# The first stage of a hybrid encoder layer: K taken by halves, four row tiles in six PSUM banks, part of the modulation as columns

## The chip, the cores and the metric

The kernel runs on one core of one Trainium2 chip. The metric is the device time of one execution in microseconds (us). Three runs of the kernel before gave 2279.6, 2280.0 and 2279.08 us; their median is 2279.6 us.

## The reference

One layer of an encoder on a sequence of 2048 rows of width 1024 (D), in float32:

```python
mod = jax.nn.silu(c) @ w_mod + b_mod              # (1, 6*1024): one row for the whole sequence
shift1, scale1, gate1, shift2, scale2, gate2 = split(mod, 6)
hmix = rms_norm(x, g_norm1) * (1.0 + scale1) + shift1
proj = hmix @ w_in          # 2832 columns: attention q, k, v, mLSTM q, k, v, o, 16 gates
...                         # banded attention, bidirectional mLSTM, output projection, gated SwiGLU FFN
```

The change concerns the first three lines and a part of the fourth: of the columns of `w_in` the first stage makes those that are wanted with rows on the partitions, the 128 of the attention's v, the 16 gates and the 512 of the mLSTM's v, 656 in all. Everything after that is the same in both kernels.

## The kernel before, in words

The 2048 rows are 16 row tiles of 128, in four groups of four (`n` from 0 to 3). A group's four x tiles are squared and summed on ACT (`squares`), their root is taken on DVE (`rsqrt`, 12 small instructions), and they are scaled by it (`scaled`). Then the group is turned: for each of the eight slices `k` of 128 columns, PE transposes four 128x128 blocks into one PSUM bank, ACT multiplies by the norm's gain and scale and adds the shift (`gs1`, `mod[:, 0, :]`, one value per partition), and DVE splits the result in a high part (float32r, rounded) and a low part, the rest (`turned`, `turned_split`). `hT[n]` holds both parts.

A product of two float32 numbers is made of three float32r matmuls: high by high, high by low, low by high (`mm3`, lines 56 to 58). `w_in`'s 656 columns are split in the same way into `wh` and `wl` (`load_nat`, `split_nat`), in two halves of K: z = 0 is k 0 to 3, z = 1 is k 4 to 7. A row tile needs 656 float32 columns of PSUM, more than the 512 of a bank, so it takes two banks, `pa` with 272 columns and `pv` with 384. A bank is named by a tag: "g", "a" and "c" have two banks each, "b" and "d" one. `nat_mm` makes one row tile: for each of the two banks, all k of its range, three matmuls each.

The modulation is needed as columns, one value per partition and k. `load_mod(m, z)` loads 512 columns of `w_mod` as four pieces of 512 KB, each with two k. `mod_sum` multiplies them by silu(c), the column `sc_col`. With `n_pe` = 4, PE takes k 0 to 3 with `sc_col` as the stationary operand, which gives one row of 512 (line 220); DVE sums k 4 to 7 in `acc`; PE adds the sum over the partitions of `acc` (line 221); ACT copies the row out (line 223), and PE turns it into four columns (line 226). With `n_pe` = 0, DVE sums all eight k and PE makes the columns from `acc` at once (line 230). `mod_bias` adds b_mod, `scales` makes `gs1`.

The order around the change: PE's instructions stay as written. ACT's, DVE's, POOL's and SP's stay as written inside the block that `pre` opens; after `pre.close()` a planner places them, and it may put later work ahead of instructions of that block where it sees them idle. SP issues nearly all loads and stores in one order, with at most eight under way. In that block, group 0 is squared, scaled and turned, in this order: modulation (1, 0) and (0, 0), `w_in`'s first half, turns of k 0 to 3, the first half of K for row tiles 0, 1 and 2 (six banks), then modulation (1, 1) and (0, 1), `w_in`'s second half, and turns of k 4 to 7. The loop over groups follows: row tiles 0 to 2 do their second half of K, and row tile 3 all of it, with a turn of group 1 after every second of its 16 steps; in group 1 a turn of group 2 stands after every eighth step. `EVERY` holds these distances. After each row tile ACT and DVE empty its banks into `vs` (one buffer, the attention's v in both parts) and `va` (two buffers), and SP stores these. `mod_row(m)`, a generator, makes the other four modulation rows; `next(vecs)` takes one half of such a row after each row tile. From line 498 on the stage with the other columns of `w_in` follows.

Of the kernel before, what the change touches and what calls it, by code (L numbers as in the profile page):

```python
# [11 lines left out]
F32 = mybir.dt.float32  # L12
F32R = mybir.dt.float32r
# [8 lines left out]
P = 128  # L22
# [14 lines left out]
def hybrid_layer_kernel(  # L37
# [125 lines left out]
    def squares(pl, xt):  # L163

        ssq = pl.tile([P, 4], F32, tag="ssq", name="ssq")
        for i in range(4):
            jk = pl.tile([P, D], BF16, tag="junk", name="junk", bufs=1)
            act.activation(jk, xt[i], AF.Square, accum_out=ssq[:, i:i + 1])
        return ssq
# [22 lines left out]

    wm_slots = deque(range(8, 16))

    def load_mod(m, z):

        r = []
        for k in range(0, KT, 2):
            w = big(wm_slots[0], "wmod", (P, 2, 512), F32)
            wm_slots.rotate(-1)  # L200
            sp.dma_start(w, w_mod[k * P:(k + 2) * P, m * D + z * 512:m * D + (z + 1) * 512]
                         .rearrange("(k p) c -> p k c", p=P))
            r.append(w)
        return r

    def mod_sum(pl, m, z, ws_, n_pe):


        acc = pl.tile([P, 512], F32, tag="macc", name="macc")
        for k in range(n_pe, KT):  # L210
            w = ws_[k // 2][:, k % 2, :]
            if k == n_pe:
                dve.tensor_scalar(acc, w, sc_col[:, k:k + 1], None, MUL)
            else:
                dve.scalar_tensor_tensor(acc, w, sc_col[:, k:k + 1], acc, MUL, ADD)
        yield True
        if n_pe:
            ps = bank("b", "modrow")
            for k in range(n_pe):
                pe.matmul(ps[:1, :], sc_col[:, k:k + 1], ws_[k // 2][:, k % 2, :], start=k == 0, stop=False)  # L220
            pe.matmul(ps[:1, :], ones[:, 0:1], acc, start=False, stop=True)
            row = pl.tile([1, 512], F32, tag="mrow", name="mrow", bufs=1)
            act.activation(row, ps[:1, :], AF.Copy)
            ps = bank("b", "modps")
            for k in range(4):
                pe.matmul(ps[:, k:k + 1], row[:, k * P:(k + 1) * P], ones[:1, 0:1], start=True, stop=True)
        else:
            ps = bank("d", "modps")
            for k in range(4):
                pe.matmul(ps[:, k:k + 1], acc[:, k * P:(k + 1) * P], ones[:, 0:1], start=True, stop=True)  # L230
        yield True
        mod_bias(m, z, ps)
        yield True

    def mod_bias(m, z, ps):
        o = O_BM + m * KT + 4 * z
        dve.tensor_tensor(mod[:, m, 4 * z:4 * z + 4], ps[:, :4], cols[:, o:o + 4], ADD)
# [40 lines left out]
    with tc.tile_pool(name="sw", bufs=2, side="right", reuse_waits="tile") as sw:  # L278
# [19 lines left out]
        wm = {(m, 0): load_mod(m, 0) for m in (1, 0)}  # L298
# [28 lines left out]
        def scales(z):  # L327
            dve.scalar_tensor_tensor(gs1[:, BD[z]], mod[:, 1, BD[z]], 1.0, cols[:, O_G1 + 4 * z:O_G1 + 4 * z + 4], ADD, MUL)

# [10 lines left out]
        def split_nat(z, r):  # L340
            ks = BD[z]
            act.activation(wh[:, ks, :144], r[0], AF.Copy)
            dve.tensor_tensor(wl[:, ks, :144], r[0], wh[:, ks, :144].bitcast(F32), SUB)
            for i in range(4):
                k, v = 4 * z + i, r[1 + i // 2][:, i % 2]
                act.activation(wh[:, k, 144:], v, AF.Copy)
                (pool, dve)[i % 2].tensor_tensor(wl[:, k, 144:], v, wh[:, k, 144:].bitcast(F32), SUB)
# [55 lines left out]

        wn = [load_nat(0)]
        wm[1, 1] = load_mod(1, 1)
        wn.append(load_nat(1))
        wm[0, 1] = load_mod(0, 1)
        xts += [load_x(1), load_x(2)]
        for src, o, n in ((g_norm2, O_G2, 8), (conv_b, O_CB, 8), (conv_w[0], O_CW, 24), (g_attn_out, O_GA, 4), (g_mlstm_out, O_GM, 4)):
            sp.dma_start(rows[1][o - N_A:o - N_A + n, :], src.rearrange("o (a b) -> (o a) b", b=P))  # L410
        hT.append(Kt(0, "hT0"))
        ms = {(m, z): mod_sum(s1, m, z, wm[m, z], 4 if m == 1 - z else 0) for z in range(2) for m in (1, 0)}
        ssq = squares(s1, xts[0])
        r = rsqrt(s1, ssq, 4, D, "rs")
        next(ms[1, 0])
        scaled(xts[0], r, True)
        next(ms[0, 0])
        next(ms[1, 0])
        next(ms[1, 0])
        next(ms[0, 0])  # L420
        next(ms[0, 0])
        scales(0)
        split_nat(0, wn[0])
        ops = {i: (bank("gga"[i], "pa"), bank("acc"[i], "pv")) for i in range(3)}
        for k in range(4):
            turned_split(s1, xts[0], k, gs1, mod[:, 0, :], hT[0])
        for i in range(3):
            deque(nat_mm(0, i, *ops[i], range(4)), 0)
        next(ms[1, 1])
        split_nat(1, wn[1])  # L430
        next(ms[1, 1])
        next(ms[1, 1])
        next(ms[0, 1])
        next(ms[0, 1])
        next(ms[0, 1])
        scales(1)
        for k in range(4, KT):
            turned_split(s1, xts[0], k, gs1, mod[:, 0, :], hT[0])
        pre.close()
        gn = cp.tile([P, 2, 2, HM, NT], F32, name="gn")  # L440
        bgv = bg.rearrange("p (d y h) -> p y d h", d=2, y=2)
        vecs = iter(())
        EVERY = ((0, 0, 0, 2), (8, 8, 8, 8), (2, 0, 0, 0), (0, 0, 0, 0))
        for n in range(NB):
# [3 lines left out]
            if n == 0:  # L448
                xts.append(load_x(3))
# [1509 lines left out]
```

## Time and profile before

| | |
|---|---|
| median of three runs | 2279.6 us |
| profiled execution: its time, its span | 2281.54 us, 2279.7 us |
| PE, DVE, ACT, POOL busy | 98%, 71%, 46%, 47% of the span |
| first matmul of the first stage (line 56) | 28.34 us |
| first matmul of row tile 4 | 78.21 us |
| first transpose inside row tile 8 | 111.98 us |
| first matmul of the next stage (line 498) | 180.92 us |

The span is the time from the first to the last instruction; the execution's own time is 1.8 us longer. Times in rows are counted from the start of the span. A row of an order in time has the start, the length, the engine, the line, the operation, what it writes and reads, its shape and the number of instructions merged into it; in square brackets stands how long the engine sat idle before it and what ended that. PEld is the loading of matmul weights, which overlaps PE. The granted clock is the share of TensorE's full clock that the chip let it have.

### The profile page before, as it was taken

The numbers are of one execution on the slowest core, as the hardware profiler recorded it, in microseconds if no ns is written. First come the engines' busy times: TensorE is split into PE (matmuls) and PEld (weight loads), VectorE is DVE, ScalarE is ACT, GpSimd is POOL, SyncE is SP. The second block draws the span as 40 slices with busy tenths as digits, with TensorE's granted clock in tenths as the row PEclk, the third lists the DMA queues.
The fourth block names the chain that finished last, engine by engine and source line by source line (L and its number), as shares of the span: only waits on it lengthen the run. The fifth ranks groups of instructions, "written<-read, shape, count | busy, mean of one in ns | idle before, by whom it ended". The sixth has DMA issues, their size and how long they took to land.

```text
span 2279.7 us, 32432 instructions
## 1 busy us (share of the span) xinstructions
PE 2225.9 (98%) x10822; PEld 1858.6 (82%) x10822; DVE 1610.1 (71%) x2931; ACT 1059.1 (46%) x2206; POOL 1067.4 (47%) x927
## 2 busy tenths in 40 slices
PE   7999999999999999999999999999999999999998
PEld 4997888888888878778888888788888888888886
DVE  6787577656688887786667786666667666785694
ACT  4433555544677746354445444433333333233352
POOL 1006535334344344436656665656566654692020
PEclk8999999999999999999999999999999999999999
DMA  8576755585666575764343454533333374442462
GB/s 323 167 246 218 231 170 163 186 242 171 201 186 183 173 251 197 265 223 147 111 157 111 157 180 147 172 98 111 97 111 97 111 253 144 166 152 93 145 216 93
DMA packets 352811, 391.28 MB, mean 172 GB/s; under 512 B 21260, under 2 KB 251004, under 8 KB 352644
## 3 DMA queue, kind: packets, MB, share of 16 engines
q1 hardware_dynamic: 352420, 389.18, 52.0%
q8 instruction: 85, 1.39, 0.2%
q14 instruction: 82, 0.67, 0.1%
q10 hardware_dynamic: 224, 0.04, 0.0%
HBM read 269.95 MB, written 119.19 MB: 171 GB/s over the span
## 4 chain that ended last, share of the span: by engine, by line
PE 51%; DVE 3%; DMA 2%; issue 1%; ACT 1%; POOL 1%; SPq 0%; ACTq 0%; DVEq 0%; POOLq 0%
PE fp L56 11%; PE fp L57 11%; PE fp L58 11%; PE fo L58 5%; PE fo L57 5%; PE fo L56 5%; PE ops L56 1%; DMA al<-a_d 1%; PE ops L58 1%; PE ops L57 1%; DVE ra L1858 1%; DVE w L1728 0%; DVE al L1719 0%; PE trn L183 0%; DMA B<-hop_d 0%
## 5 line engine op out<-in xcount | busy, mean ns | idle before, releaser
L498 PE MATMUL gps<-hT,whi 128*128 128x512 f32 x1088 | 396.2, 419 | 0.3 <-DVE cacc L513 0.3
L57 PE MATMUL fo<-w,ah 128*128 128x512 f32 x616 | 239.8, 389 | 1.6 <-DVE w L1728 1.6
L58 PE MATMUL fo<-w,al 128*128 128x512 f32 x616 | 239.8, 389 | 0.3 <-DVE al L1719 0.3
L56 PE MATMUL fo<-w,ah 128*128 128x512 f32 x616 | 239.7, 389 | 0.0
L498 PE MATMUL gps<-hT,wlo 128*128 128x512 f32 x544 | 226.6, 416 | 0.0
L498 PEld LDWEIGHTS gps<-hT,whi 128*128 128x128 f32 x1088 | 199.8, 190 | 24.4 <-DVE cacc L513 0.7
L56 PE MATMUL fp<-T,S 128*128 128x512 f32 x528 | 206.9, 392 | 2.9 <-ACT s L1615 2.9
L57 PE MATMUL fp<-T,S 128*128 128x512 f32 x528 | 205.7, 390 | 0.0
L58 PE MATMUL fp<-T,S 128*128 128x512 f32 x528 | 205.4, 389 | 0.0
L1719 DVE TENSOR_TENSOR al<-al,ah 128x1024 fp32r<-128x1024 f32 x77 | 116.8, 1521 | 112.9 <-ACT ah L1718 112.7
L1718 ACT ACTIVATE ah<-al 128x1024 fp32r<-128x1024 f32 x77 | 81.6, 1060 | 188.9 <-DMA al<-a_d 183.7
L1458 DVE TENSOR_TENSOR S<-sf,S 128x512 fp32r<-128x512 f32 x86 | 129.6, 1545 | 39.4 <-ACT S L1457 39.2
L1458 DVE TENSOR_TENSOR A<-graw,A 128x512 fp32r<-128x512 f32 x86 | 129.4, 1526 | 14.5 <-ACT A L1457 14.5
L1623 DVE SCALAR_TENSOR_TENSOR g<-t,g 128x512 f32<-128x512 f32 x44 | 44.2, 1005 | 132.6 <-ACT t L1622 132.6
L57 PEld LDWEIGHTS fo<-w,ah 128*128 128x128 f32 x616 | 115.6, 188 | 26.2 <-DVE w L1728 2.0
L58 PE MATMUL fp<-B,A 128*128 128x512 f32 x352 | 136.9, 389 | 0.0
L56 PE MATMUL fp<-B,A 128*128 128x512 f32 x352 | 136.9, 389 | 0.0
L57 PE MATMUL fp<-B,A 128*128 128x512 f32 x352 | 136.9, 389 | 0.0
L58 PEld LDWEIGHTS fo<-w,al 128*128 128x128 f32 x616 | 115.6, 188 | 24.7 <-DVE al L1719 0.7
L56 PEld LDWEIGHTS fo<-w,ah 128*128 128x128 f32 x616 | 115.6, 188 | 24.0
L1462 POOL TENSOR_TENSOR sf<-A,A22r 128x512 f32<-128x512 f32 x43 | 61.3, 1427 | 154.8 <-DMA A22r<-in_w_ffn_in_dram 121.2
L798 POOL TENSOR_SCALAR ap<-ap,adn 128x384 f32<-128x384 f32 (+1 forms) x128 | 71.1, 574 | 123.3 <-PE atp L805 62.8
(418 smaller groups left out, 6168.5 us busy)
## 6 DMA issues: line engine op xcount, KB each, us to landing
al<-a_d SPq DMA_DIRECT2D x77, 512.0 KB, 3.7
wmod<-in_w_mod_dram SPq DMA_DIRECT2D x48, 512.0 KB, 7.6
graw<-in_w_ffn_in_dram SPq DMA_DIRECT2D x43, 512.0 KB, 3.7
a_d<-ka SPq DMA_DIRECT2D x66, 256.0 KB, 4.6
bc<-bc_d SPq DMA_DIRECT2D x64, 256.0 KB, 3.6
hop_d<-n SPq DMA_DIRECT2D x56, 256.0 KB, 4.5
a_d<-u SPq DMA_DIRECT2D x55, 256.0 KB, 4.5
mqk<-qk_d SPq DMA_DIRECT2D x44, 256.0 KB, 4.0
```

The source lines that it names most:

```text
L56: pe.matmul(o, lh, rh, start=first, stop=False, skip_group_check=skip)
L57: pe.matmul(o, lh, rl, start=False, stop=False, skip_group_check=skip)
L58: pe.matmul(o, ll, rh, start=False, stop=last, skip_group_check=skip)
L498: pe.matmul(ps, w[i == 2][:, k, :], hT[n](i == 1, k), start=(k == 0 and i == 0), stop=(k == KT - 1 and i == 2))
L798: pool.tensor_scalar(self.p[g][:, :self.NK], self.p[g][:, :self.NK], dn[:, g:g + 1], 0.0, MUL, ADD)
L1458: dve.tensor_tensor(t[:, 1, :], f, t[:, 0, :].bitcast(F32), SUB)
L1462: pool.tensor_tensor(f1, a21, a22, ADD)
L1623: dve.scalar_tensor_tensor(g0, t0, 1.0, g0, ADD, MUL)
L1718: act.activation(ah, al.bitcast(F32), AF.Copy)
L1719: dve.tensor_tensor(al, al.bitcast(F32), ah.bitcast(F32), SUB)
L1858: dve.tensor_tensor(ra[i], ra[i], xr, ADD)
```

## The change

Four things in the block that `pre` opens, which now reaches to the end of row tiles 4 and 5:

- `Four` does four row tiles of group 0 at once with K outside: for each k, the four tiles, three matmuls for each of two banks. Tiles 2p and 2p + 1 share a bank "g", with 272 columns of the even and 240 of the odd tile; the even tile's other 384 columns stand in a bank "a", the odd tile's other 416 in a bank "c". So four tiles take six banks, and two remain for transposes. Tiles 4 and 5 are done in the same way (`two`), with group 1's transposes two k ahead (`turns`).
- `Mod` replaces `load_mod`, `mod_sum`, `mod_bias` and `scales`. Some k are summed on DVE (`sums`); for others PE has a block of `w_mod` as the stationary operand and `sc_col` as the one moving column, four matmuls for each k (`products`), and the four columns are added up in PSUM; `close` adds the DVE sum with four more matmuls and then b_mod. Blocks (1, 0) and (0, 0) take k 4 to 7 on PE, block (1, 1) none, block (0, 1) k 5 to 7.
- ACT writes the high part of a turned column directly and the whole value in a second instruction (`turned_hi`); DVE makes only the low part. In groups 2 and 3 this stays as it was. The low part of `w_in` is made on DVE alone (`nat_lo`), not half on POOL, and group 0's scaling is shared by ACT and DVE.
- The loads are in another order: `w_in`'s first half before modulation (0, 0); x of groups 1 and 2 after all of these; x of group 3 after the last transposes of group 0. Evacuation and stores are functions of their own (`leave`, `keep`). Groups 2 and 3 follow in the old loop; row tiles 6 and 7 have a turn after every fourth step.

The diff, cut to its core:

```diff
+    def turns(xt, k, tag):
+        ps = bank(tag, "trn")
+        for i in range(4):
+            pe.transpose(ps[:, i * P:(i + 1) * P], xt[i][:, k * P:(k + 1) * P], ident)
+        return ps
+    def turned_hi(pl, ps, k, gs, shift, dst):
+        act.activation(dst(0, k), ps, AF.Identity, bias=shift[:, k:k + 1], scale=gs[:, k:k + 1])
+        t = pl.tile([P, 512], F32, tag="ntmp", name="ntmp", bufs=2)
+        act.activation(t, ps, AF.Identity, bias=shift[:, k:k + 1], scale=gs[:, k:k + 1])
+        return t
+    def turned_lo(t, k, dst):
+        dve.tensor_tensor(dst(1, k), t, dst(0, k).bitcast(F32), SUB)
...
+    class Mod:
...
+        def product(self, w, col, tag, last=False):
+            for j in range(4):
+                first = self.ps is None
+                if first:
+                    self.ps = bank(tag, "modps")
+                pe.matmul(self.ps[:, j:j + 1], w[:, j * P:(j + 1) * P], col, start=first, stop=last, skip_group_check=True)
+        def products(self, ks, tag):
+            for k in ks:
+                self.product(self.w[k // 2][:, k % 2, :], sc_col[:, k:k + 1], tag)
...
+        class Four:
+            def __init__(self, n, pairs):
+                self.n, self.o = n, {}
+                for p in pairs:
+                    x, y, z = bank("g", "pa"), bank("a", "pv"), bank("c", "pv")
+                    self.o[2 * p] = ((x[:, :272], slice(0, 272)), (y[:, :384], slice(272, 656)))
+                    self.o[2 * p + 1] = ((x[:, 272:512], slice(0, 240)), (z[:, :416], slice(240, 656)))
+            def mm(self, i, k):
+                for j, (o, cs) in enumerate(self.o[i]):
+                    lh, ll = (hT[self.n](s, k, slice(i * P, (i + 1) * P)) for s in (0, 1))
+                    mm3(o, lh, ll, wh[:, k, cs], wl[:, k, cs], k == 0 and (j == 1 or i % 2 == 0), k == KT - 1, True)
...
+        m10 = Mod(1, 0)
         wn = [load_nat(0)]
-        wm[1, 1] = load_mod(1, 1)
+        m00 = Mod(0, 0)
...
+        ssq = squares(s1, x0)
+        m10.sums(s1, (0, 1))
+        r = rsqrt(s1, ssq, 4, D, "rs")
...
+        m10.sums(s1, (2, 3))
+        m10.products(range(4, 8), "c")
+        m10.close("c")
+        m11 = Mod(1, 1)
+        nat_hi(0, wn[0])
+        nat_lo(0, wn[0], (0, 1))
+        trn = {k: turns(x0, k, "bd"[k]) for k in range(2)}
+        m00.sums(s1, range(4))
+        m00.products(range(4, 8), "c")
+        m00.close("c")
+        wn.append(load_nat(1))
+        m01 = Mod(0, 1)
+        four = Four(0, (0, 1))
...
+        for k in range(2):
+            high(k)
+            low(k)
+        for i in range(4):
+            four.mm(i, 0)
+        nat_lo(0, wn[0], (2, 3))
+        m11.sums(s1, (0, 1))
+        trn[2] = turns(x0, 2, "b")
+        high(2)
+        low(2)
+        for i in range(4):
+            four.mm(i, 1)
+        m11.sums(s1, (2, 3, 4, 5))
...
+        four.mm(0, 3)
+        m11.close("b")
+        xts.append(load_x(1))
...
+        xts.append(load_x(2))
+        m01.sums(s1, range(5))
+        four.mm(1, 3)
+        trn[4] = turns(x0, 4, "b")
+        m01.products(range(5, 8), "d")
+        m01.close("d")
...
+        for o in ((0, 6), (1, 6), (0, 7)):
+            four.mm(*o)
+        trn[0] = turns(x1, 0, "b")
+        four.mm(1, 7)
+        high1(0)
+        low1(0)
+        keep(0, *leave(0, *four.outs(0)))
+        trn[1] = turns(x1, 1, "d")
+        for o in ((2, 6), (2, 7)):
+            four.mm(*o)
+        keep(1, *leave(1, *four.outs(1)))
+        high1(1)
+        low1(1)
+        for o in ((3, 6), (3, 7)):
+            four.mm(*o)
+        two = Four(1, (0,))
+        for k in range(KT):
+            for i in range(2):
+                two.mm(i, k)
+                if i == 0 and k + 2 < KT:
+                    trn[k + 2] = turns(x1, k + 2, "bd"[k % 2])
+            if k < 2:
+                keep(k + 2, *leave(k + 2, *four.outs(k + 2)))
+            if k + 2 < KT:
+                high1(k + 2)
+                low1(k + 2)
         pre.close()
-        EVERY = ((0, 0, 0, 2), (8, 8, 8, 8), (2, 0, 0, 0), (0, 0, 0, 0))
-        for n in range(NB):
+        EVERY = ((), (0, 0, 4, 4), (2, 0, 0, 0), (0, 0, 0, 0))
+        for n in range(1, NB):
```

More of the change, by code (lines that the diff above doesn't have):

```diff
@@ L429, in hybrid_layer_kernel @@
[L429 to L438, printed above, removed]
+        xts.append(load_x(2))
[4 more added lines that the diff above has]
+        m01.close("d")
+        four.mm(2, 3)
@@ new lines, in hybrid_layer_kernel @@
+        trn[5] = turns(x0, 5, "d")
+        four.mm(3, 3)
+        x1 = xts[1]
+        ssq = s1.tile([P, 4], F32, tag="ssq", name="ssq")
+        some_squares(s1, x1, ssq, (0, 1))
+        for k in (4, 5):
+            high(k)
+            low(k)
+        nat_lo(1, wn[1], (2, 3))
+        for i in range(4):
+            four.mm(i, 4)
+        some_squares(s1, x1, ssq, (2, 3))
+        trn.update({k: turns(x0, k, "bd"[k % 2]) for k in (6, 7)})
+        xts.append(load_x(3))
+        for i in range(4):
+            four.mm(i, 5)
```

191 lines of the change are left out of this document (102 added, 89 removed).

## The prediction

> **What bounds the kernel now.** I read the page first (busy shares, slices), then the busy time by stretches, then the order in time of PE, DVE and ACT up to 112 us, then the landing times.
>
> ```profile
> span 2279.7 us, 32432 instructions
> ...
> PE 2225.9 (98%) x10822; PEld 1858.6 (82%) x10822; DVE 1610.1 (71%) x2931; ACT 1059.1 (46%) x2206; POOL 1067.4 (47%) x927
> ...
> PE   7999999999999999999999999999999999999998
> ...
> PEclk8999999999999999999999999999999999999999
> ```
>
> PE is full in every slice but the first, so what the first stage gains or loses reaches the end one for one; no later stage has a hole to take it up.
>
> ```profile
> 20.00:30.00 10.00, 6.86 (x37) 5.60 (x37) 8.75 (x15) 5.10 (x8) 3.09 (x2) 0.73 1.09 388
> ...
> 28.34:78.28 49.94, 47.29 (x268) 41.12 (x268) 38.97 (x98) 29.89 (x56) 3.68 (x6) 0.90 0.67 244
> 78.28:111.90 33.62, 33.20 (x225) 32.64 (x225) 25.70 (x54) 9.64 (x20) 0.42 (x4) 1.00 0.52 175
> ```
>
> Columns: length; busy PE, PEld, DVE, ACT, POOL; granted clock; DMA share; GB/s. The changed part ends at 78.28, where four of sixteen row tiles and two of four groups of transposes are done. 28.34 to 78.28 has a clock of 0.90 and modulation work; from 78.28 on the stage runs at full clock with 0.4 us of PE idle.
>
> ```profile
> 11.74 6.56 PE L220 MATMUL modrow<-wmod,sc_col 128*1 128x512 f32 x8 [6.15 <-DVE rsy L101]
> 23.09 1.05 PE L230 MATMUL modps<-ones_r,macc 128*128 128x1 f32 x8 [2.20 <-DVE macc L215]
> 28.34 0.59 PE L56 MATMUL pa<-wnh,hT 128*128 128x272 f32 x1 [0.28 <-DVE hT L190]
> 36.87 0.29 PE L56 MATMUL pa<-wnh,hT 128*128 128x272 f32 x1
> 37.24 0.33 PE L56 MATMUL pv<-wnh,hT 128*128 128x384 f32 x1
> 37.77 0.34 PE L56 MATMUL pv<-wnh,hT 128*128 128x384 f32 x1
> 43.83 3.59 PE L220 MATMUL modrow<-wmod,sc_col 128*1 128x512 f32 x8
> ```
>
> ```profile
> 26.15 1.50 PEld L183 LDWEIGHTS trn<-ident,xt 128*128 128x128 f32 x7
> 50.26 0.86 PEld L183 LDWEIGHTS trn<-ident,xt 128*128 128x128 f32 x8 [0.34 <-DVE mod L237]
> ```
>
> Prices on PE. Per row tile and k: three matmuls 272 wide in 0.37 us (36.87 to 37.24), three 384 wide in 0.53: 0.90. At half clock everything doubles: L220 costs 6.56 against 3.59, eight transposes 1.72 against 0.86. A 128x1 product is two records (x8 for four), about 0.22 us at full clock; all of that is its weight load, since one column streams nothing.
>
> ```profile
> 11.37 0.17 DVE L99 TENSOR_SCALAR rsv<-ssq 128x4 f32<-128x4 f32 x1 [5.25 <-ACT junk L168]
> 13.35 0.16 DVE L106 SCALAR_TENSOR_TENSOR rsy<-rsa,rsy 128x4 f32<-128x4 f32 x1
> 14.23 0.49 DVE L213 TENSOR_SCALAR macc<-wmod,sc_col 128x512 f32<-128x512 f32 x1 [0.72 <-DMA wmod<-in_w_mod_dram]
> 17.56 5.47 DVE L215 SCALAR_TENSOR_TENSOR macc<-wmod,sc_col,macc 128x512 f32<-128x512 f32 x7
> 28.31 0.69 DVE L191 TENSOR_TENSOR hT<-ntmp,hT 128x512 fp32r<-128x512 f32 x1
> 58.53 2.74 DVE L177 TENSOR_SCALAR xt<-xt,rsy 128x1024 f32<-128x1024 f32 x4
> ```
>
> ```profile
> 13.55 4.27 ACT L175 ACTIVATE xt<-xt,rsy 128x1024 f32<-128x1024 f32 x4 [2.21 <-DVE rsy L106]
> 21.82 0.68 ACT L342 ACTIVATE wnh<-wnr 128x576 fp32r<-128x576 f32 x1 [2.02 <-DMA wnr<-in_w_in_dram]
> 22.99 2.38 ACT L346 ACTIVATE wnh<-wnr 128x512 fp32r<-128x512 f32 x4 [0.49 <-DMA wnr<-in_w_in_dram]
> 25.28 1.43 ACT L184 ACTIVATE ntmp<-trn,mod,gs 128x512 f32<-128x512 f32 x2
> 57.01 0.26 ACT L478 ACTIVATE vs<-pa 128x128 fp32r<-128x128 f32 x1
> 59.40 0.49 ACT L482 ACTIVATE va<-pv 128x384 f32<-128x384 f32 x1
> 64.12 1.06 ACT L168 ACTIVATE junk<-xt 128x1024 bf16<-128x1024 f32 x1
> 65.30 1.06 ACT L168 ACTIVATE junk<-xt 128x1024 bf16<-128x1024 f32 x1
> ```
>
> DVE: 0.49 for the first and 0.77 for each further modulation sum, 2.1 for a root (11.37 to 13.5), 0.69 for a low half. ACT: 0.72 per write of a turned column, 1.18 per square with its readout (64.12 to 65.30), 1.07 per scaled tile.
>
> **The change part by part.** I compare one point: tiles 0 to 5 done and groups 0 and 1 turned. Before, that is 78.28 plus two tiles of 8 x 0.90 = 92.7.
>
> *Loads.* The first half of w_in (1.34 MB) passes the second modulation block. Before, the first wnr piece, right behind that block, landed at 21.8, so the block was there about 21.1; 1.34 MB at 388 GB/s make it 24.5. This costs nothing: PE is still at the block before.
>
> *Modulation as columns.* Removed: the 1-row products (L220, L221, L226), 6.56 us and more per block. Added: 16 products and 4 closing ones for the two first blocks each, 4 and 16 for the later two. The first waits for the third wmod piece (14.2, the DMA wait above). PE has no dense work before it, so I price it at half clock: the nearest rows are the weight loads, 0.21 each at 26.15 and 0.11 at 50.26, which makes 0.44 per product. 16 products 14.2 to 21.3, closing 23.0; the first eight transposes 24.8; the second block's 16 products 31.8, closing 33.6. The sums on DVE (done 28.4), the w_in halves on ACT (20.3) and DVE lie beside. DVE adds the bias, ACT writes the high half: first matmul 34.7, its low half 36.1. **Before it was 28.34.** Ends: 0.22 per product gives 28.9 (the load at 24.5 then bounds); 0.44 gives 34.7. I take the second; clock 0.73 in 20:30, after a stretch of small matmuls, is the nearest row.
>
> *K outside, four tiles.* A k is 4 x 0.90 = 3.6. Before, PE was at full pace by 36.87, 8.5 us after its start; I take half clock until 40, then full: k=0 ends 41.8, with the next transposes (0.45) k=1 45.9, k=2 49.9. High half and full value both come from ACT (1.43 instead of 0.72 and a DVE cast), the low half from DVE: 2.1 us after the transposes, hidden under a k. Moving w_in's two low parts per half from POOL to DVE adds 2 x 0.69 (as L191), hidden too. Two modulation sums now stand before group 0's root (1.3), and DVE takes two of its four scalings from ACT: both end by 17.2, under the products.
>
> *Second modulation half.* DVE does 8 sums of block m11 around the low halves, then w_in's low halves (2.1), then five sums: 56.1. PE meanwhile does one tile's k=3, 12 products (2.7), waits 0.4, closes at 57.0; scale and shift at 57.2; k=4 begins 59.3, ends 62.9; the last transposes of group 0 end at 63.8, k=5 at 67.4. PE spends 4.5 us on products here; before, L220 alone took 3.59 (43.83).
>
> *ACT from 57.2.* In the changed program's instruction order the planner has pulled work into the set order: ACT does two columns (2.9), two squares of group 1 (2.35), four of group 2 (4.7), then columns 6 and 7 (2.9): 70.1. PE wants column 6 at 67.4 and gets its low half at 69.6: 2 us lost. Then two scaled tiles (2.1), **four squares of group 3 (4.7)**, and only then group 1's first column: 78.4. Group 3's load cannot start before 63.8, as it takes group 0's buffers:
>
> ```profile
> DMA to landing us min/median/max: 3.5/6.6/11.0
> ```
>
> (x tiles to 60 us), so it is there by 71; ACT, not the load, is late. On SP the stores of tiles 0 to 3 stand behind it, but they are due from 79 on. PE finishes tile 3 at 77.7.
>
> *Six banks.* Tiles 4 and 5 take the banks of tiles 0 and 1, so their first matmul waits for both evacuations. These stand on ACT behind the column at 78.4, and tile 1's vs write waits for tile 0's store, as vs has one buffer:
>
> ```profile
> DMA to landing us min/median/max: 1.7/5.2/5.8
> ```
>
> (vst_d stores). DVE does the root (1.7 after the squares), the low half (79.4), vs, four scaled tiles of group 3 (2.7), then vs of tile 1 at 83.3. PE starts tile 4 at 83.9, **6.2 us idle**. The next columns follow the evacuations of tiles 1, 2, 3 one by one on ACT (1.4 each with 1.0 to 1.6 of evacuation): column 3's low half 93.6, k=3 done 95.6. The clock lost in the gap is hidden under this. From there PE bounds: four k of 1.80 and three transposes of 0.45 make 104.
>
> *The rest.* Tiles 6 and 7 carry four turns each instead of tiles 4 to 7 two each: the same sum. Rows of mod_row(2) come one tile later, their wmod pieces wait for group 1's turns (about 101) and are summed before tile 6 ends: nothing.
>
> The narrow matmuls: odd tiles take 240 and 416 columns for 272 and 384. Nearest rows for a narrow float32r operand:
>
> ```profile
> 587.66 0.31 PE L783 MATMUL as<-ak,aq 128*128 128x256 f32 x1
> 587.78 0.62 PE L498 MATMUL gps<-hT,whi 128*128 128x512 f32 x1
> ```
>
> 256 wide: 0.12 start to start. No row is below 256. Lower end 0.11 (the weight load); upper end plain f32, L220: 3.59/4 for 512 columns, so 0.42 for 240. I take 0.115, nearest to the 256 row.
>
> Sum: 104 - 92.7 = +11.3. The profiled execution took 2281.5 us (span 2279.7), so 2292.8 for it; the runs' median, 2279.6, lies 1.9 lower: **2290.6**. A measurement here tells no change from one of about 0.2%, 4.6 us.
>
> **The rivals.** *Products at full price.* If their weight loads are not slowed, or the products themselves raise the clock, the first matmul comes at 28.9 and the same steps end at 98.2: +5.5, **2285**. Against it: weight loads double at 26.15. The Trainium skill, TensorE: Matmul & The Clock Gate, LDWEIGHTS, gives columns/1.2 ns whatever the clock, so 107 ns, and by that rule this rival would hold; the trace's 0.21 against 0.11 disagrees.
>
> *Narrow matmuls slow.* At 0.42 each of 72 matmuls costs 0.3 more: 14.6 us in eight k and 7.3 in tile 5, of which ACT's lateness hides some 11: +22, **2302**; with the full-price rival +17. For it: nothing below 256 columns exists before. Against: 256 shows no step.
>
> *PE is not starved in tiles 4 and 5* (the other side). If ACT has written group 1's first columns and both evacuations by the time tile 3 ends, the loop takes 8 x 1.80 + 6 x 0.45 = 17.1 from 77.7: 94.8, +2.1, **2281.7**, no slower than can be told. It decides when the column that I put at 78.4 comes before 72. With a start at 28.9 it would be 72.2 + 17.1 = 89.3: -3.4, 2276. For it: ACT had idle time in this stretch before (29.9 busy of 49.9). Against: the instruction order.
>
> **How the numbers follow.** Forecast 0.30 (own range 2286 to 2295), full price 0.22, narrow slow 0.25, not starved 0.23. Slower by over 0.2%: forecast, narrow, 0.13 of full price: 0.68. Faster: 0.13 of the last, where several of its waits vanish with an early start. The same: 0.19. The range reaches from the last rival's early start to the narrow one: 2276 to 2302.
>
> **What would show it.** First pa matmul at 34.7, and twenty L242 products spaced 0.44 per pair of records; a PE wait of 2 us at k=6 and one of 6 us before tile 4, with ACT squares ahead of it; 240-wide starts 0.115 apart; the tile 8 starting at 123 against 111.9. The prediction is wrong if PE enters tile 4 without a wait, or if 240-wide matmuls stand 0.4 apart.

## The result and the profile after

The changed kernel is slower: 2292.0 us (median; 2288.1 to 2296.0) against 2279.8 us for the kernel before on the same chip. The ratio is 1.0048, with a 95% interval of 1.0038 to 1.0058. The forecast was 2290.6 us.

The first three lines and the clock line of the profile's page, changed kernel. Span 13.5 us longer, and PE full from the second slice on, as before:

```profile
span 2293.2 us, 32554 instructions
...
PE 2233.0 (97%) x10890; PEld 1878.2 (82%) x10890; DVE 1606.8 (70%) x2916; ACT 1068.7 (47%) x2223; POOL 1062.1 (46%) x923
...
PE   7899999999999999999999999999999999999998
...
PEclk9999999999999999999999999999999999999999
```

Where it is lost is read at three points that both kernels pass. The first matmul of the stage starts at 34.62 (28.34 before). Tiles 4 and 5 end at 104.20 (the forecast worked out 92.7 for the same state before). The first matmul of the gate projection starts at 194.67 (180.92 before). So the change is 6.3, then 11.5, then 13.8 us late, and from there on the distance stays (13.5 at the end of the span). The rows of PE's order in time, changed kernel:

```profile
25.02 6.83 PE L242 MATMUL modps<-sc_col,wmod 128*128 128x1 f32 x32
31.71 1.85 PE L242 MATMUL modps<-ones_r,macc 128*128 128x1 f32 x8
34.62 0.60 PE L56 MATMUL pa<-wnh,hT 128*128 128x272 f32 x1 [1.06 <-ACT hT L205]
...
50.81 0.95 PE L242 MATMUL modps<-ones_r,macc 128*128 128x1 f32 x8
...
56.46 1.84 PE L242 MATMUL modps<-ones_r,macc 128*128 128x1 f32 x8
...
67.49 0.28 PE L56 MATMUL pa<-wnh,hT 128*128 128x240 f32 x1
67.60 0.27 PE L57 MATMUL pa<-wnl,hT 128*128 128x240 f32 x1
...
71.88 0.39 PE L58 MATMUL pa<-wnh,hT 128*128 128x272 f32 x1 [1.21 <-DVE hT L211]
...
85.11 0.60 PE L56 MATMUL pa<-wnh,hT 128*128 128x272 f32 x1 [5.08 <-ACT va L457]
...
104.20 0.26 PE L327 MATMUL colps<-ident,rows 48*128 48x48 f32 x1
```

Sixteen products of m00 (32 records) take 6.83 us, 0.43 each. The same four closing products cost 1.85 us at 31.7, 0.95 at 50.8 and 1.84 at 56.5: the price doubles with the halved clock. The 240-wide matmuls start 0.11 us apart. PE waits 1.21 us at k=6 and 5.08 us ahead of tile 4. ACT's order says who is late (here L172 are the squares, L205 the first write of a turned column):

```profile
58.54 0.78 ACT L205 ACTIVATE hT<-trn,mod,gs 128x512 fp32r<-128x512 f32 x1 [5.73 <-DVE mod L252]
...
62.38 1.05 ACT L172 ACTIVATE junk<-xt 128x1024 bf16<-128x1024 f32 x1
...
69.34 0.76 ACT L205 ACTIVATE hT<-trn,mod,gs 128x512 fp32r<-128x512 f32 x1
...
74.07 1.06 ACT L172 ACTIVATE junk<-xt 128x1024 bf16<-128x1024 f32 x1
...
78.67 0.76 ACT L205 ACTIVATE hT<-trn,mod,gs 128x512 fp32r<-128x512 f32 x1
...
83.16 0.28 ACT L452 ACTIVATE vs<-pa 128x128 fp32r<-128x128 f32 x1 [1.02 <-DMA vst_d<-vs]
```

Column 4 comes at 58.5, six squares push column 6 to 69.3, the four of x3 push group 1's first column to 78.7, and the evacuation of tile 1 starts at 83.2. Last, the stretch from tiles 4 and 5 to the gate projection, by windows, after and before (length; busy PE, PEld, DVE, ACT, POOL; clock; DMA share; GB/s):

```profile
104.20:194.67 90.47, 86.11 (x564) 82.02 (x564) 76.31 (x169) 31.93 (x65) 6.07 (x16) 1.00 0.68 224
```

```profile
92.70:180.92 88.22, 85.43 (x560) 81.92 (x559) 69.21 (x150) 30.13 (x60) 6.52 (x15) 1.00 0.61 199
```

It is 2.3 us longer (90.47 against 88.22), and DVE has 7.1 us more work in it. The greater part of that is mod_row(2): half of such a row is eight sums of 0.5 to 0.8 us. Before, the first half's sums began at 81.00 and ended ahead of this stretch, now they begin at 103.37 (DVE's order, before and after):

```profile
81.00 0.49 DVE L373 TENSOR_SCALAR macc<-wmod,sc_col 128x512 f32<-128x512 f32 x1 [0.55 <-DMA wmod<-in_w_mod_dram]
```

```profile
103.37 0.49 DVE L392 TENSOR_SCALAR macc<-wmod,sc_col 128x512 f32<-128x512 f32 x1 [1.43 <-DMA wmod<-in_w_mod_dram]
```

What PE waits for in this stretch is not these sums at once. Its longest wait there is for ACT, and ACT's is for the store of `vs`, which has one buffer (ACT's order and PE's, changed kernel):

```profile
118.15 0.28 ACT L452 ACTIVATE vs<-pa 128x128 fp32r<-128x128 f32 x1 [3.88 <-DMA vst_d<-vs]
118.32 0.77 ACT L187 ACTIVATE ntmp<-trn,mod,gs 128x512 f32<-128x512 f32 x1
```

```profile
119.15 0.66 PE L186 MATMUL trn<-ident,xt 128*128 128x128 f32 x4 [1.46 <-ACT ntmp L187]
```

### The profile page after: what moved, and what is told of

Read it like the earlier page. It is cut to its first block, busy times and chain, and to the rows that moved or that the text cites. A ratio compares the mean times of both kernels' runs of the same rounds, so it can differ in the third digit from the quotient of the medians.

```text
span 2293.2 us, 32554 instructions
## 1 busy us (share of the span) xinstructions
PE 2233.0 (97%) x10890; PEld 1878.2 (82%) x10890; DVE 1606.8 (70%) x2916; ACT 1068.7 (47%) x2223; POOL 1062.1 (46%) x923
## 4 chain that ended last, share of the span: by engine, by line
PE 51%; DVE 3%; DMA 2%; issue 1%; ACT 1%; POOL 1%; SPq 0%; ACTq 0%; POOLq 0%; DVEq 0%
PE fp L56 11%; PE fp L57 11%; PE fp L58 11%; PE fo L58 5%; PE fo L57 5%; PE fo L56 5%; DMA al<-a_d 1%; DVE al L1859 1%; PE ops L56 1%; PE ops L58 1%; PE ops L57 1%; DVE w L1868 1%; DVE ra L1998 0%; DMA T<-hop_d 0%; PE trn L186 0%
```

## The experiments

All are edits of the changed kernel, compared with the kernel before on the same chip; "before" has the 92.7 that was worked out. The marks (us from the span's start) come from the profiled execution of each; the ratio with its 95% interval from several.

| | first matmul | tile 4 starts (wait) | tiles 4, 5 end | gate projection | time over before |
|---|---|---|---|---|---|
| before | 28.34 | 78.21 | 92.7 | 180.92 | 1 |
| the change | 34.62 | 85.11 (5.08) | 104.20 | 194.67 | 1.0048 [1.0038, 1.0058] |
| the change, again | 34.41 | 84.89 (5.08) | 103.98 | 193.57 | 1.0058 [1.0046, 1.0071] |
| dense work | 35.70 | 86.17 (5.12) | 105.26 | 195.51 | 1.0057 [1.0045, 1.0069] |
| late x3 | 34.09 | 79.81 (0.32) | 104.49 | 194.98 | 1.0058 [1.0045, 1.0071] |
| two vs | 34.39 | 82.87 (3.14) | 102.16 | 190.78 | 1.0036 [1.0024, 1.0048] |
| early squares | 34.48 | 80.32 (3.97) | 99.42 | 191.08 | 1.0039 [1.0027, 1.0051] |
| sums on DVE | 30.79 | 78.70 (5.08) | 97.98 | 189.80 | 1.0049 [1.0033, 1.0065] |
| all squares | 34.32 | 79.57 (0.26) | 98.67 | 191.57 | 1.0040 [1.0026, 1.0054] |
| m01 | 34.52 | 83.23 (5.41) | 102.46 | 192.79 | 1.0043 [1.0029, 1.0057] |
| three terms | 30.84 | 74.59 (0) | 93.21 | 183.36 | 1.0002 [0.9993, 1.0011] |
| four terms | 30.03 | 74.62 (0) | 94.81 | 187.65 | 1.0022 [1.0013, 1.0031] |
| early rows | 30.70 | 74.88 (0) | 105.01 | 191.77 | 1.0033 [1.0020, 1.0046] |
| early rows, start | 29.88 | 73.67 (0) | 101.53 | 188.24 | 1.0030 [1.0018, 1.0042] |

Executions of one kernel spread by up to 9.4 us, so a single term of 2 to 6 us is surer in the marks than in the ratio.

The marks have a second cause beside each edit, the clock. Between 50 us and the end of tile 5 it was at half for 13.7 us in the change (both executions) and in m01, for 10.2 us in late x3, two vs, sums on DVE and all squares, and for 6.8 us in early squares, the three terms and the four terms, always in stretches of 3.4 us or a multiple. Since work on PE takes twice as long there, each 3.4 us costs up to 1.7 us. A difference of that size between two marks can be the clock alone.

**The change, again.**

> The changed kernel itself, once more, beside the variants of it on the same chip. Every theory: the time is that of the kernel before plus 0.4 to 0.6%, with a spread of some 6 us between executions; first matmul at 34.6, wait ahead of tile 4 of 5 us. If the spread comes from single half-clock stretches of 3.4 us far behind the changed part (at about 600 and 836 us in the profile of the changed kernel), this profile shows the same ones or fewer, and its time differs by about 1.7 us for each.

The marks repeat within 0.3 us up to tile 5. The spread may come in part from single half-clock stretches far behind the changed part. By windows, at the first of these places: the change, the change again, the kernel before, and the variant with early squares:

```profile
601.10:604.50 3.40, 3.40 (x13) 3.05 (x14) 1.74 (x7) 1.79 (x6) 0.00 (x0) 0.53 1.06 318
```

```profile
600.00:603.40 3.40, 3.40 (x14) 2.92 (x13) 2.05 (x9) 1.89 (x7) 0.00 (x0) 0.51 0.98 293
```

```profile
587.80:591.20 3.40, 3.40 (x14) 2.92 (x13) 2.07 (x9) 1.90 (x7) 0.00 (x0) 0.50 1.08 327
```

```profile
594.00:600.00 6.00, 3.90 (x22) 3.11 (x21) 2.69 (x12) 2.14 (x8) 0.00 (x0) 1.00 1.08 325
```

Three of four have it; the fourth has PE idle for 2.1 of 6 us there and keeps its clock. The kernel before has it as well, so it is no part of the answer. Both profiled executions of the changed kernel have the same two such stretches (near 600 and 836 us) and lie only 0.7 us apart. So they don't test whether stretches of this kind make the spread, and the 8 us between the executions of the changed kernel stay open.

**Dense work ahead of the products.**

```diff
+        wz = big(0, "wz", (P, 512))
+        dve.memset(wz.bitcast(F32), 0.0)
...
+        dense(24)
...
         trn = {k: turns(x0, k, "bd"[k]) for k in range(2)}
+        dense(12)
```

`dense(n)` is n matmuls 128x512 of the tile of zeros `wz`; the 24 stand ahead of m10's products.

> The changed kernel, with 24 dense 128x512 matmuls of a tile of zeros on PE ahead of m10's products and 12 more behind the first eight transposes; their results are read by nobody, nothing else is changed. Theory (the working of the forecast: a 128x1 product costs 0.43 us because the clock is granted at half while PE does little, and 0.22 at full): with the clock raised before the products, m00's column products take some 7 us in place of 14, the first matmul of k=0 starts at about 29 us in place of 34.6, the columns k = 0 and 1 lose their half-clock part, and the kernel is 4 to 6 us shorter than the changed one (about 2287). Rival (a product has its price whatever the clock, or the clock is not raised by 9 us of dense work): the first matmul stays within 1 us of 34.6 and the time stays within 1.5 us of the changed kernel's.

By windows of the products alone (line 242), busy PE and clock, and PE's order:

```profile
15.70:18.00 2.30, 2.23 (x20) 1.00 1.06 389
...
18.50:20.60 2.10, 2.10 (x11) 0.50 1.03 385
```

```profile
28.77 4.17 PE L242 MATMUL modps<-sc_col,wmod 128*128 128x1 f32 x32
...
35.70 0.60 PE L56 MATMUL pa<-wnh,hT 128*128 128x272 f32 x1 [1.06 <-ACT hT L205]
```

The price follows the clock: 20 records in 2.23 us at full clock (0.11 each, 0.22 a product), 11 in 2.10 at half, with some records missing. The rival that a product costs the same whatever the clock is dead. But the theory's gain did not come, and the time is the change's, as the rival had it: the products do not hold the clock. It fell 2.3 us after they began, so the second dense block ran mostly at half clock, took 4.9 us (23.91 to 28.77), and gave back 2.7 (4.17 for m00's products in place of 6.83). The start came 1.1 us later.

**x3 loaded late.**

```diff
-        xts.append(load_x(3))
         for i in range(4):
             four.mm(i, 5)
...
                 low1(k + 2)
+        xts.append(load_x(3))
         pre.close()
```

> The changed kernel, with the load of the fourth row of x (x3) issued behind the loop that ends with tiles 4 and 5 instead of ahead of tile 3's last column. Theory (the forecast's: the four squares of x3 stand ahead of group 1's first column on ACT, 74.1 to 78.4 us, and so delay the evacuation of tiles 0 and 1): without the load there the squares move behind the columns, group 1's first column is ready at about 74.5 instead of 79.4, the wait of 5.1 us ahead of tile 4 falls to 0.5 to 2 us, and tiles 4 and 5 end 3 to 4.5 us earlier; the total is 2 to 4.5 us shorter if norm of tile 12 to 15 is not late for it, and about the same if it is. Rival (tile 4 waits for the evacuation of tiles 0 and 1 through the one buffer vs, and the squares only fill ACT's idle time): the wait stays above 4 us and the total within 1.5 us of the changed kernel's.

PE's order and ACT's:

```profile
79.81 0.39 PE L56 MATMUL pa<-wnh,hT 128*128 128x272 f32 x1 [0.32 <-ACT va L457]
...
94.46 0.39 PE L56 MATMUL pa<-wnh,hT 128*128 128x272 f32 x1 [1.36 <-ACT hT L205]
```

```profile
91.21 1.06 ACT L172 ACTIVATE junk<-xt 128x1024 bf16<-128x1024 f32 x1 [2.06 <-DMA xt<-in_x_dram]
```

The wait ahead of tile 4 went from 5.08 to 0.32 us, so the work on x3 made it. The edit moves x3's squares on ACT and its scaling on DVE (2.74 us from 81.74, between the evacuations of tiles 0 and 1) together and does not part them. Nothing was won: the planner put the squares between group 1's columns 4 and 6, the first waited 2.06 us for the load, and PE now waits 5.6 us in six places inside tiles 4 and 5.

**Two buffers for vs.**

```diff
-            vs = sw.tile([P, KV, 2, HD], F32R, tag="vs", name="vs", bufs=1)
+            vs = sw.tile([P, KV, 2, HD], F32R, tag="vs", name="vs")
```

> The changed kernel, with two buffers for vs in place of one, so that the evacuation of tile 1 does not wait for the store of tile 0's vs. Theory (the forecast's: the order of ACT and DVE ahead of tile 4 is the limit, and the buffer adds the 1.0 us that stands ahead of ACT's second write of vs): tile 4 starts 0 to 1.2 us earlier, and the total is 0 to 1.2 us shorter. Rival (the one buffer is what holds tile 4): the wait of 5.1 us falls below 2.5 us and the total falls by 2.5 us or more.

The wait fell by 1.94 us and tiles 4 and 5 end 2.0 us earlier, between the two expectations: with the 1.02 us for the store went a part of ACT's next wait for DVE as well (1.36 us at 84.80 in the changed kernel, 0.51 us here). It is a second cause beside the work on x3, not the first.

By the gate projection the gain is 3.9 us, for the stretch behind is shorter too (by windows):

```profile
102.16:190.78 88.62, 85.90 (x564) 81.91 (x564) 75.91 (x169) 31.66 (x65) 6.52 (x16) 1.00 0.72 229
```

That is 0.4 us more than before the change, with PE idle for 2.7 us as before (2.8; in the changed kernel 4.4), though the sums of mod_row(2) are as late as in the changed kernel (from 101.64) and DVE is as busy. The wait of 1.46 us is gone. This points to the one vs buffer as what turns late work on DVE into a loss on PE there.

**Early squares.**

```diff
...
-        some_squares(s1, x1, ssq, (0, 1))
+        some_squares(s1, x1, ssq, range(4))
+        ssq2 = s1.tile([P, 4], F32, tag="ssq", name="ssq")
+        some_squares(s1, xts[2], ssq2, (0, 1))
         for k in (4, 5):
             high(k)
             low(k)
...
-        some_squares(s1, x1, ssq, (2, 3))
+        some_squares(s1, xts[2], ssq2, (2, 3))
...
```

> The changed kernel, with ACT's squares for the norms of groups 1 and 2 taken earlier: all four of x1 and two of x2 ahead of columns 4 and 5, in ACT's idle 5.7 us before m01's columns are ready, and the other two of x2 behind column 5. Theory (the forecast's: six squares between columns 5 and 6 make column 6 late, which PE meets as the wait of 1.2 us at k=6, and with the four squares of x3 and the scaling make group 1's first column late): column 6 is written about 4 us earlier (65 to 66 in place of 69.3), PE's waits at k=6 (0.3 + 1.2 us) go, group 1's first column comes 1 to 3 us earlier, and the total is 1.5 to 3.5 us shorter than the changed kernel's. Rival (PE is late at k=6 for its own transposes and the slower clock, and tile 4 waits for the evacuation): only the 1.5 us at k=6 move, tile 4 waits that much longer, and the total stays within 1 us.

ACT's order: column 6, then group 1's first.

```profile
64.21 0.78 ACT L205 ACTIVATE hT<-trn,mod,gs 128x512 fp32r<-128x512 f32 x1 [2.22 <-PE trn L200]
...
73.56 0.76 ACT L205 ACTIVATE hT<-trn,mod,gs 128x512 fp32r<-128x512 f32 x1
```

Column 6 now waits for PE, not PE for it, and both columns come 5.1 us earlier. Tiles 4 and 5 end 4.8 us earlier, more than expected; up to 1.7 us of that are the clock's, as the half-clock stretch around m01 was 3.4 us in place of 6.8 in this execution. The rival is dead.

**Sums on DVE.**

```diff
-        m10.sums(s1, (2, 3))
-        m10.products(range(4, 8), "c")
-        m10.close("c")
+        m10.sums(s1, range(2, 7))
+        m10.products((7,), "c")
...
         nat_lo(0, wn[0], (0, 1))
+        m10.close("c")
...
-        m00.sums(s1, range(4))
-        m00.products(range(4, 8), "c")
+        m00.sums(s1, range(7))
+        m00.products((7,), "c")
```

> The changed kernel, with seven of eight rows of the first two modulation blocks (m10, m00) summed on DVE and one multiplied as columns on PE, in place of four and four, and with w_in's first two low parts ahead of m10's closing addition on DVE. Theory (the forecast's: 16 products of 0.43 us behind the landing of m00 at 24.5 make the first matmul 6 us later than before): 4 products end at 26.2, the seven sums on DVE at about 27.5, the close at 29.3, the first matmul comes at 30 to 31 in place of 34.6, and the total is 3 to 4.5 us shorter than the changed kernel's. Rival (m01's close, from DVE's sums and the loads, sets column 4 and with it all that follows): the first matmul moves as above, but the wait ahead of k=4 grows by as much, and the total is within 1.5 us of the changed kernel's.

PE's order:

```profile
24.29 1.87 PE L242 MATMUL modps<-sc_col,wmod 128*128 128x1 f32 x8 [0.20 <-DMA wmod<-in_w_mod_dram]
27.86 1.86 PE L242 MATMUL modps<-ones_r,macc 128*128 128x1 f32 x8 [1.70 <-DVE macc L235]
30.79 0.60 PE L56 MATMUL pa<-wnh,hT 128*128 128x272 f32 x1 [1.07 <-ACT hT L205]
...
78.70 0.59 PE L56 MATMUL pa<-wnh,hT 128*128 128x272 f32 x1 [5.08 <-ACT va L457]
```

The start comes 3.8 us earlier, and tile 4 6.4. All follows the start, also ACT's squares, and the wait of 5.08 stays; the clock gives the rest. From the first matmul to the next transposes PE took 6.3 us in place of 7.2, and the half-clock stretch around m01 was 3.4 us in place of 6.8. The rival is dead by the marks. The ratio does not show the gain (1.0049, the rival's total); the five executions lay between 2288.8 and 2298.2 us, the profiled one at 2290.2.

**All squares out of the way.** The edit of early squares, and the four of x3 one by one behind group 1's columns 4 to 7:

```diff
...
                 high1(k + 2)
                 low1(k + 2)
+            if 2 <= k < 6:
+                some_squares(s1, xts[3], ssq3, (k - 2,))
...
```

> The changed kernel, with all three sets of squares out of the way of the columns on ACT: those of x1 and two of x2 ahead of columns 4 and 5 (as in the earlier variant), and the four of x3 one by one behind group 1's columns 4 to 7, where ACT had about 0.8 us idle per column. Theory (the forecast's: the squares of x3 ahead of group 1's first column are the larger part of the wait ahead of tile 4): that column is written as soon as its transposes are done, at 71 to 72 in place of 79.4 (73.6 + 0.8 with the earlier squares alone), tile 4 starts at 76.5 to 78.5 in place of 85.1 (80.3 with the earlier squares alone), the wait ahead of it is 0 to 2 us, and tiles 4 and 5 end at 95.5 to 97.5 in place of 104.2; total 5 to 8 us shorter than the changed kernel's. Rival (the store of tile 0's vs and DVE's scaling of x3 hold the evacuation, whatever ACT does): tile 4 starts at 79.5 or later, and the total is 3 to 5 us shorter, as with the earlier squares alone.

ACT's order and PE's:

```profile
74.36 0.78 ACT L205 ACTIVATE hT<-trn,mod,gs 128x512 fp32r<-128x512 f32 x1 [2.32 <-PE trn L200]
```

```profile
79.57 0.39 PE L56 MATMUL pa<-wnh,hT 128*128 128x272 f32 x1 [0.26 <-ACT va L457]
```

The column waits for its transposes and PE hardly waits for the evacuation. By its numbers the rival came out (tile 4 at 79.57, the time about 4 us under the change's), but not by its reason, for nothing holds the evacuation any more. Group 1's transposes themselves came later than I expected (10 us of half clock from 53.9 in this execution), so the marks moved less: tiles 4 and 5 end 5.5 us earlier. By the gate projection only 3.1 of these are left; the stretch behind is 92.9 us.

**m01.** Seven of its rows on DVE behind column 3, close behind all of k=3:

```diff
-        m11.sums(s1, (6, 7))
+        m11.close("b")
+        m01.sums(s1, range(7))
...
-        m01.products(range(5, 8), "d")
+        m01.products((7,), "d")
```

> The changed kernel, with seven of eight rows of m01 summed on DVE (five before), directly behind column 3's low half, m11's sums moved up into DVE's idle time ahead of column 2's low half, and m01's closing products behind all of k=3 on PE instead of inside it. Theory (the second modulation half holds k=4: in the changed kernel PE spends 5.3 us on m01's products and close, partly at half clock, and column 4 is first written at 58.5): column 4 is written at 55.5 to 56.5, PE has nothing to do for 3 to 4 us ahead of k=4 where it did products, and tiles 4 and 5 end 2 to 3 us earlier (101 to 102 in place of 104); total 1.5 to 3 us shorter than the changed kernel's. Rival (the squares on ACT set columns 6, 7 and group 1's first, so that an earlier column 4 is worth nothing): column 4 as above, but tiles 4 and 5 end within 1 us of 104.

```profile
57.72 0.78 ACT L205 ACTIVATE hT<-trn,mod,gs 128x512 fp32r<-128x512 f32 x1 [5.62 <-PE trn L200]
```

Column 4 (ACT's order, above) moved by 0.8 us, not 2 to 3: m11's bias now stands ahead of the sums on DVE and waits 2.24 us for PE's closing products. Tiles 4 and 5 end 1.7 us earlier. Neither theory is decided.

**Three terms together:** sums on DVE, all squares, two vs.

> All that helped together: seven of eight rows of m10 and m00 summed on DVE, the squares out of the way of the columns, two buffers for vs. Theory (the three delays of the forecast add up: start 4 us, squares 6 to 7, vs buffer 1 to 2): tiles 4 and 5 end at 91 to 94 in place of 104.2, and the total is 10 to 13 us shorter than the changed kernel's, within 3 us of the kernel before. Rival (one of them is hidden behind m01's products at half clock or behind the loads): tiles 4 and 5 end at 95 to 98, and the total is 6 to 9 us shorter, still 3 us or more above the kernel before.

By windows, tiles 4 and 5's end to the gate projection:

```profile
93.21:183.36 90.15, 86.17 (x564) 82.01 (x564) 78.29 (x180) 32.13 (x65) 6.97 (x16) 1.00 0.69 225
```

Tiles 4 and 5 end 11.0 us earlier, with no wait ahead of tile 4, and the time is that of the kernel before: 1.0002 [0.9993, 1.0011]. This is the main proof that these three make the loss up to tile 5. The terms alone make 6.2, 5.5 and 2.0, in sum 2.7 more; as the half-clock stretches differ between these executions, it is not shown that the terms overlap. The stretch behind, which the forecast took to be unchanged, is still 2 us longer than before: here vs has two buffers, but DVE has even more to do in it (78.3 us).

**Four terms.** The same with m01 as above, squares of x2 later, and two of m00's sums ahead of m10's bias.

> The combination that equalled the kernel before (start, squares, vs buffers), with m01 as in the variant beside it, the sums of m00 partly in DVE's idle time ahead of m10's bias, and the squares of x2 spread so that group 1's first columns are not behind them. Theory (the three terms still add, and the second modulation half is a fourth): first matmul at 29 to 30 (30.8 in the combination), column 4 written at 49.5 to 51.5 (54.8), tiles 4 and 5 end at 86.5 to 89.5 (93.2); total 3 to 6 us shorter than that combination, 2 to 5 us under the kernel before. Rival (ahead of k=4 PE only waits where it did products, and ACT or the loads of m01, x1 and x2 set the columns from there): tiles 4 and 5 end at 91 to 93.5, and the total is within 2 us of the combination's.

ACT's order (column 4) and PE's:

```profile
54.14 0.78 ACT L205 ACTIVATE hT<-trn,mod,gs 128x512 fp32r<-128x512 f32 x1 [4.41 <-DVE mod L252]
```

```profile
118.23 0.33 PE L186 MATMUL trn<-ident,xt 128*128 128x128 f32 x1 [1.86 <-DVE xt L180]
```

The theory fell. Column 4 came at 54.1 (54.8 in the three terms). The later squares of x2 put DVE's scaling of x2 (89.1 to 92.4) among group 1's last low halves, and PE waits 0.60 and 0.52 us for these. Behind that DVE is late with the scaling of x3 too: the row at 118.23 is a transpose of group 3.

**Early rows of mod_row(2).** On top of the three terms; `mod_row` hands over behind each piece of two rows, and `next(vecs)` takes one such piece:

```diff
-        wrow = deque(["big24", "big25", "big26", "big27"])
+        wrow = deque(["big16", "big17", "big18", "big19"])
...
+        vecs = mod_row(2)
         two = Four(1, (0,))
...
                 low1(k + 2)
+            next(vecs)
```

> The combination that equalled the kernel before (start, squares, vs buffers), with the first half of mod_row(2)'s sums done earlier: its pieces go to four buffers that are free once w_in's first half is split, and DVE adds one piece of two rows behind each of group 1's columns 2 to 5, where it had 1.6 to 2.3 us idle per column; in the combination all sixteen sums stand behind tile 5. Theory (the forecast's step that mod_row(2) one tile later costs nothing is wrong: DVE, busy 21.7 of 21.8 us from 93.2 to 115, holds tiles 6 to 8): the first tile behind the group-3 transposes and all from there come 1 to 2.5 us earlier against the end of tile 5, the stretch from tiles 4 and 5's end to the first gate projection falls from 90.1 us to 88 to 89 (88.1 before the change), and the total is 1 to 2.5 us shorter than the combination's, at or just below the kernel before. Rival (the scaling of x2 and x3 and the turned columns hold DVE there, whatever the sums do, or the sums now delay group 1's low halves): the stretch stays within 0.7 us of 90.1, or tiles 4 and 5 end later by what it loses.

> The same as the variant beside it, with the sums of m00 partly in DVE's idle time ahead of m10's bias (first matmul at 30.0 in place of 30.8, as seen in the variant with four terms). Theory: the 0.8 us go through to the end, and the total is 0.5 to 1 us below the variant beside it; together 1.5 to 3.5 us below the combination's. Rival (m01's close is set by DVE's sums and the loads, not by the start): column 4 is written when it was, and the two totals agree within 0.4 us.

DVE's order, then the stretch by windows, first variant:

```profile
82.74 0.49 DVE L392 TENSOR_SCALAR macc<-wmod,sc_col 128x512 f32<-128x512 f32 x1 [2.91 <-DMA wmod<-in_w_mod_dram]
...
91.47 1.54 DVE L394 SCALAR_TENSOR_TENSOR macc<-wmod,sc_col,macc 128x512 f32<-128x512 f32 x2 [4.21 <-DMA wmod<-in_w_mod_dram]
```

```profile
105.01:191.77 86.76, 84.72 (x563) 81.59 (x562) 72.74 (x164) 31.62 (x64) 6.56 (x16) 1.00 0.67 217
```

Both the theory's stretch and the rival's price came true; the total grew instead of falling. With half of the sums gone from it, the stretch falls from 90.15 to 86.76 us, below the 88.22 before the change. This points to the sums as what holds tiles 6 to 8 in the three terms. It is not a clean price, for tiles 4 and 5 end 11.8 us later. There DVE waits for pieces whose loads stand behind the stores on SP, with group 1's low halves behind it. PE waits 5.4 us more than in the three terms, and 13.7 us of half clock make most of the rest. In the variant with the earlier start column 4 comes 0.7 us earlier (53.81 for 54.54), so its rival is dead. That it ends tiles 4 and 5 3.5 us earlier is for the greater part the clock, at half for 6.8 us there in place of 13.7.

## Why the prediction was right

**Right, by its steps.** First matmul 34.7: 34.62. A product 0.44: 0.43. Ends of k=0 and 1 at 41.8 and 45.9: the transposes behind them stood at 41.81 and 45.85. A lost stretch at k=6 for column 6 behind six squares: 1.2 us where 2 were given. Group 1's first column behind the squares of x3, done at 78.4: begun at 78.67 and done at 80.1, so 1.7 us late. A wait of 6.2 us ahead of tile 4: 5.08, and all squares out of the way left 0.26. Tiles 4 and 5 done at 104: 104.20. 240-wide matmuls 0.115 apart: 0.11. The vs buffer as a part of the wait: 1.94 us. The last transposes ahead of tile 8 at 123: 124.30 (the row at 111.98 before is group 2's eighth turn, at the end of tile 7, and so is this one).

**The price of a product.** In one execution of the changed kernel four closing products took 0.95 us at full clock and 1.84 at half. The Trainium skill, TensorE: Matmul & The Clock Gate, LDWEIGHTS, gives one formula for a weight load, with no clock in it. By it the rival "Products at full price" would have held; the measurement decides. Single half-clock stretches last 3.4 us here (the windows above). The Trainium skill, on the same page under Part 1: The HAM clock gate, says that a free-running window of some 3.4 us decides on the clock. This case agrees as to the length.

**Wrong in size.** "*Second modulation half*" took full clock for m01's products and for what follows them. The products brought it down again: the close at 56.46 took 1.84 us, column 4's low half was there at 60.7, not 59.3, k=4 began at 62.1, and tile 3 ended at 80.0, not 77.7. This met a wait ahead of tile 4 that was 1.1 us shorter, and 19.1 us for tiles 4 and 5 in place of 20.1. So the sum of 104 came out almost exactly, but by errors that cancel, which is luck.

**Wrong: "*The rest ... nothing*".** I let mod_row(2) come later for free because its sums would end within tile 6. The first half's sums do, but they stand ahead of the evacuations on DVE, where before they were done ahead of this stretch. The stretch to the gate projection is 2.3 us longer in the profiled execution and 1.4 in the second (193.57 less 103.98 is 89.6). The cover that I had not named was the vs buffer: I counted it ahead of tile 4 only, and behind tile 5 it makes ACT wait 3.88 us and PE 1.46 (in the second execution ACT waits 1.66 us there, and PE does not). With two buffers and the sums as late, the stretch is 88.6 us against 88.2. These are single executions, so the share of each cause in the 2.3 us stays open. The three terms, which have two buffers, lose 2 us there all the same, with DVE fuller; the early rows point to the sums for that, but don't part them from what else moved. The 11.5 us at tile 5 and these 2.3 make the 13.8 at the gate projection. The forecast's sum was 11.3; the profiled executions lie 13.7 apart (2295.2 against 2281.5), the medians 12.2.

**The rivals.** Full price and narrow matmuls are dead by the rows above. "PE is not starved" was wrong for this order of instructions, and became true when the squares were moved: the three terms start tile 4 without a wait. Its gain below the kernel before (2276) never came, as the start was still 2.5 us later than before and the stretch behind tile 5 was 2 us longer.

## What to carry to other kernels

Before work is moved to a resource that looks idle, price it at the state that the resource is in there: small products on a PE that does nothing else cost twice, and bring the clock down for what follows. When a set order is written by hand, list what the planner may still put into it; here, ten squares of 1.2 us on an engine that is busy for 47% of the span: with them out of the way (and DVE's scaling of x3 with them), 5.5 of the 11.5 us lost by tile 5 came back. And a step that becomes late "for free" needs slack on the engine that does it and in the buffers behind that engine, not only in its load.

## What the runs showed of the hardware

Twenty-four dense matmuls raised the clock, and it fell 2.3 us after the 128x1 products began. PE had been idle for 1.4 us just ahead of these, but the second time it was not: m00's products began at 28.77 right behind twelve dense matmuls, at full clock, and it fell to half at 31.7. In this case back-to-back products of one column don't hold the clock. In the changed kernel the clock column of the windows has 1.00 for the first 20 us of products,

```profile
14.76:34.62 19.86, 18.80 (x88) 18.71 (x89) 8.47 (x18) 5.84 (x9) 0.00 (x0) 1.00 1.07 396
```

while each of them takes the half-clock price (0.43 us against 0.22): here, at the start of the span, the spacing of equal instructions tells more than that column. And PE idle for 2.1 us near 600 us was followed by a half-clock stretch of 3.4 us in the changed kernel, and by none in the variant with early squares.
